# Squares of x summed on TensorE, decay and beta columns as one stationary tile with two passes, softmax sums spread by transposes

## The chip, the cores and the metric

The kernel runs on one core of one Trainium2 chip. The metric is the device time of one execution in microseconds; the kernel before takes 911.56 us (median of 3 runs, 911.46 to 915.03). The profile is that of one execution, taken by the hardware profiler.

## The reference, cut to what matters

One layer of a diffusion backbone, in f32, for 512 latent tokens and 256 context tokens of width 1024. The parts that the change touches:

```python
def rms_norm(x, g):
    xf = x.astype(jnp.float32)
    return xf * lax.rsqrt(jnp.mean(xf * xf, axis=-1, keepdims=True) + EPS) * g.astype(jnp.float32)
...
    h = rms_norm(x, g_norm1) * (1.0 + sc1) + sh1
    hc = rms_norm(ctx, g_norm1) * (1.0 + csc1) + csh1
    aq, ak, av, dq, dk, dv, dz, da, db, ga, gd = split_cols(h @ w_in)
...
        beta = jax.nn.sigmoid(pb.reshape(pb.shape[0], T, N_DIR, DN_HEADS))
        g = -jnp.exp(a_log) * jax.nn.softplus(pa.reshape(pa.shape[0], T, N_DIR, DN_HEADS) + dt_bias)
...
    p = jax.nn.softmax(jnp.concatenate([s_loc, s_ctx, s_sink], axis=-1).astype(jnp.float32), axis=-1)
```

`da` and `db` (16 columns each of the input projection) give the decay g and the rate beta of the gated DeltaNet branch. Behind these come the DeltaNet scans in both directions, windowed attention, gates, an output projection and an MLP.

## The kernel before, in words

Activations lie transposed: 128 features on the partitions, tokens along the free axis, eight feature tiles `kt`. Products of f32 precision are made of three matmuls in a faster 32-bit format: each weight w and each activation x is split in a high part (a cast on ScalarE) and a low part (the difference, on VectorE), and `mm3` (L288 to L296) adds whi·xhi (L293), whi·xlo (L294) and wlo·xhi (L295) into one PSUM accumulator. Matmuls on plain f32 operands (the sums of squares L332 and L676, the modulation products L228, the broadcasts L634) run as two passes each in the trace.

**The start.** 30 matmuls of `ones` on `ones` (L209) keep TensorE busy while the first loads land. The four pieces of `xT` (128x1024 each, two feature tiles) land one after the other. `norm1` (L315) squares each on ScalarE (L319), adds the four on VectorE (L325), folds 1024 to 512 columns (L329) and sums over the partitions with one matmul with `ones` (L332); logarithm and exponential (both at L164) give 1/rms. `ada(kt)` (L220) makes the modulation columns of one feature tile from two halves of `wada1` (L228); `columns` (L241) evicts them (L244), turns them (L249) and writes `modA` and `modS` (L257, L258). `features(kt)` (L341) calls `modulate` (L298): scale on VectorE (L299), shift and high part on ScalarE (L300), low part on VectorE (L301). The context goes through `norm1` too, with two pieces.

**The early tiles.** While the columns of the eight feature tiles come in, three output tiles of the input projection are accumulated k by k: T_AB (decay and beta: 16 columns of `da`, 16 of zeros, 16 of `db`, and 80 of zeros) and the first two DeltaNet key tiles T_DK and T_DK+1. `load_early` (L282) loads and splits their weights. Per k and tile there are three matmuls of 512 columns and three of 256 (latent and context tokens). Then follow the tiles T_DK+2 and T_DK+3, whose weights are loaded and split by `wload` (L263: cast L271, low part L276), and behind them the `selq` matmuls (L734). The accumulator of T_AB is read from PSUM by L697 (add of the bias `dtb`) and L699 (exponential of beta); a chain of logarithms and exponentials on 16 partitions ends in `gb` (L707), which the `selq` matmuls (L734) read. The key tiles are read by `conv` (L655: ScalarE L658, VectorE L659, L660).

**Attention.** For each of eight (query block, kv head) units, `scores` and `outputs` run. `outputs` transposes the probabilities (L613), splits them, multiplies with the values (L602, L603), and then multiplies the result by the inverse softmax sums: for each of four heads, a matmul (L634) with the sums' column, broadcast to 128 columns, as stationary operand, and the identity gives a 128x128 block with the sums along the free axis; VectorE multiplies (L635).

The order of the instructions on each engine is set when the kernel is built, by a scheduler that goes by data dependences, buffers and its own estimate of times; an engine then works through its list in order. `follow` (L198) adds single orderings by hand.

Of the kernel before, what the change touches and what calls it, by code (L numbers as in the profile page):

```python
# [8 lines left out]
F32 = mybir.dt.float32  # L9
F32R = mybir.dt.float32r  # L10
BF16 = mybir.dt.bfloat16
AF = mybir.ActivationFunctionType
# [24 lines left out]
P = 128  # L37
# [24 lines left out]
UPOS, SPOS = [UORD.index(q) for q in range(4)], [SORD.index(q) for q in range(4)]  # L62


T_AK, T_AV, T_AQ, T_AB = 0, 1, 2, 6
T_DK, T_DV, T_DQ, T_DZ = 7, 11, 15, 19
T_GA, T_GD = 23, 31
N_IN = 39

# [41 lines left out]
def tile_layer(ctx: ExitStack, tc: tile.TileContext, I: dict, out: bass.AP, dbg=None):  # L113
# [42 lines left out]
    def act(out_, in_, func, **kw):  # L156

        sets = TABLES.get(func)
        if sets and actg["set"] not in sets:
            head = A.preload_act_table_set(sets[0])  # L160
            for o in actg["ops"]:
                tc.add_manual_dep(head.ins, o.name, nosync, reason="table sets")
            actg.update(set=sets[0], head=head.ins, ops=[head.ins])
        r = A.activation(out_, in_, func, **kw)  # L164
        if sets:
            tc.add_manual_dep(r.ins, actg["head"].name, nosync, reason="table sets")
            actg["ops"].append(r.ins)
        return r
# [110 lines left out]
    early, EARLY = [], {T_AB: 0, T_DK: 0, T_DK + 1: 0}  # L279
    ebufs = []  # L280

    def load_early():  # L282
        bb = alloc(1024), alloc(1024)
        ebufs.extend(bb)
        early.append((wload(I["win"][list(EARLY)[len(early)]], bufs=bb), bank(2)))


    def mm3(acc, w, xs, start=True, stop=True, ks=None):  # L288
        ks = list(range(len(xs))) if ks is None else ks
        n = len(ks)  # L290
        for i, k in enumerate(ks):
            xhi, xlo = xs[i]
            PE.matmul(acc, w[0][:, k, :], xhi, start=(start and i == 0), stop=False)  # L293
            PE.matmul(acc, w[0][:, k, :], xlo, start=False, stop=False)  # L294
            r = PE.matmul(acc, w[1][:, k, :], xhi, start=False, stop=(stop and i == n - 1))  # L295
        return r  # L296

    def modulate(t, src, r, sc, sh, hi, lo, eng=V):  # L298
# [55 lines left out]
        return mm3(acc[:, :512], w, [hx[k]], start=(k == 0), stop=(k == KT - 1), ks=[k])  # L354


    normed = [norm1(xs_, 4, SEQ, rx)]
    follow(w0, normed[0])
    columns(0, rp0)
    features(0)  # L360
# [228 lines left out]
    def outputs(qb, kv):  # L589

        b0, b1, nb, n = span(qb)
        probs, pks = pkd[qb, kv][:2]
        pv = bank()
        cols = [b0 + b for b in range(nb)] + [4, 5]
        last = None

        def values():
            i0, vs, ph = last
            for x, vo in enumerate(vs):
                i = i0 + x  # L600
                v = r32(VS[:, vo * 256 + kv * P:vo * 256 + (kv + 1) * P])
                PE.matmul(pv.ap, v, r32(ph[0][:, x * 512:x * 512 + 512]), start=(i == 0), stop=False)  # L602
                PE.matmul(pv.ap, v, r32(ph[1][:, x * 512:x * 512 + 512]), start=False, stop=(i == len(cols) - 1))  # L603
            for b in ph:
                b.free()

        for i0 in range(0, len(cols), 2):
            vs = cols[i0:i0 + 2]
            m = len(vs) * 512
            pt = bank(len(vs))  # L610
            for x in range(len(vs)):
                for j in range(4):
                    PE.transpose(pt[:, x * 512 + j * P:x * 512 + (j + 1) * P], probs[j][:, (i0 + x) * P:(i0 + x + 1) * P], ident)  # L613
            ph = alloc(m), alloc(m)
            split(pt.ap, ph[0].ap, ph[1].ap)
            pt.free()
            if last:
                values()
            last = i0, vs, ph
            yield  # L620
        values()
        for p in pks:
            p.free()
        if kv == 0:
            yab[qb] = alloc(512)
        ya, r = yab[qb], own[kv]
        A.activation(ya[r], pv[own[1 - kv]], AF.Copy)
        V.tensor_tensor(ya[r], ya[r], pv[r], op=ALU.add)
        pv.free()

        st = pkd.pop((qb, kv))[2]
        rb = bank()
        for j in range(4):
            PE.matmul(rb[:, j * P:(j + 1) * P], st[:, 2, j:j + 1].broadcast_to([P, P]), ident, start=True, stop=True)  # L634
        V.tensor_tensor(ya[r], ya[r], rb[r], op=ALU.mult)  # L635
        rb.free()
        if kv == 1:
            split(ya.ap, Q[0][:, qb].rearrange("p j t -> p (j t)"), Q[1][:, qb].rearrange("p j t -> p (j t)"))
            ya.free()
        yield  # L640
# [53 lines left out]

    t, t2 = alloc(TOK), alloc(TOK)
    ad, mx, be = t[0:16], t2[0:16], gb[32:48]
    V.tensor_scalar(ad, acc[0:16, :TOK], dtb[0:16], None, op0=ALU.add)  # L697
    V.tensor_scalar(mx, ad, 0.0, None, op0=ALU.max)
    act(be, acc[32:48, :TOK], AF.Exp, scale=-1.0)  # L699
    acc.free()  # L700
    act(be, be, AF.Ln, bias=onec[32:48])
    act(be, be, AF.Exp, scale=-1.0)
    A.activation(ad, ad, AF.Abs)
# [980 lines left out]
def pack(i):  # L1684
# [21 lines left out]
    wbd = i["w_br_dn"][0].reshape(8, HD, D)[heads].reshape(512, D)  # L1706
    aqp = aq.reshape(D, 2, 4, HD).transpose(0, 2, 1, 3).reshape(D, 512)
    z16 = np.zeros((D, 16), np.float32)
    ab = np.concatenate([da, z16, db, z16, np.zeros((D, 64), np.float32)], 1)
    a["win"] = blk(np.concatenate([ak, av, aqp, ab, dk, dv, dq, dz, ga, gd], 1))  # L1710
    wba = i["w_br_attn"][0].reshape(2, 4, HD, D).transpose(1, 0, 2, 3).reshape(512, D)
    a["wbr"] = np.stack([blk(wba), blk(wbd)])
    a["wout"] = blk(i["w_out"][0])
# [10 lines left out]
    prm[:, 67:75] = i["attn_sink"][0][None]  # L1724
    prm[:, 75:111] = i["conv_w"][0].reshape(3, 12, P).transpose(2, 1, 0).reshape(P, 36)
    prm[0:16, 111] = i["a_log"][0].reshape(-1)
    prm[0:16, 112] = i["dt_bias"][0].reshape(-1)

    sel = np.zeros((64, 2, 5, 4, 2), np.float32)
    for n, (kind, places, order) in enumerate(((0, ZP, range(4)), (1, ZP, range(4)), (0, UP, UORD), (1, UP, UORD), (0, (0,) * 4, range(4)))):  # L1730
# [27 lines left out]
```

## Time and profile before

| | |
|---|---|
| median of 3 runs | 911.56 us |
| span of the profiled execution | 909.7 us |
| TensorE, weight loads, VectorE, ScalarE busy | 96%, 79%, 72%, 55% |
| loads | 103.87 MB read, 2.10 MB written, mean 116 GB/s |

The span is from the first to the last instruction of the profiled execution; the profile has no time of its own for that execution beside it, and the median of the timed runs is 1.9 us above the span. A matmul's start is exact, its end is modelled, so TensorE's rate is read from start to start. A row of the timeline gives start, duration, engine, line, operation, output<-inputs, shape, count, and in brackets the idle time before it with what ended it. "L293" is line 293 of the kernel before. A row of the chain of waits gives start, length and what was waited for. A row of the busy time by stretch gives, for each engine, busy time and count, then the granted TensorE clock, the share of the DMA engines, and GB/s.

### The profile page before, as it was taken

What the parts mean: (1) busy time and instruction counts of PE and PEld (TensorE: products, weight loads), DVE (VectorE), ACT (ScalarE), POOL (GpSimd) and SP (SyncE); (2) the same over time, 40 slices, a digit from 0 to 9 for tenths busy, and PEclk for the clock granted to TensorE, in tenths of its full rate; (3) what the DMA queues carried; (4) which work ended last, traced back from release to release, by engine and by line L of the source; (5) the groups of instructions that cost most, each with busy time, mean ns of one, the idle gap of its engine ahead of it and who ended that gap; (6) DMA issues with size and microseconds to landing.
All of it is one profiled execution on the core that took longest, in us unless ns stands there. A gap on an engine that the chain in (4) does not pass through costs nothing.

```text
span 909.7 us, 18033 instructions
## 1 busy us (share of the span) xinstructions
PE 873.9 (96%) x7564; PEld 721.3 (79%) x7564; DVE 652.9 (72%) x1111; ACT 496.9 (55%) x881; POOL 26.0 (3%) x42
## 2 busy tenths in 40 slices
PE   8999999989999998889999999999999999999998
PEld 6688667867777676656677789888898899889986
DVE  5665799876778999566666968896587567837631
ACT  6368764475768795475654434463265246424520
POOL 0000001010000001100000000000000000000000
PEclk9999999999999999999999999999999999999999
DMA  9824455532311136523143645453412332334031
GB/s 355 312 76 117 94 131 107 113 73 47 57 36 35 59 121 235 182 67 99 49 152 107 241 127 186 155 170 115 139 48 93 116 116 70 116 93 139 1 116 46
DMA packets 31985, 107.13 MB, mean 118 GB/s; under 512 B 4000, under 2 KB 4512, under 8 KB 31904
## 3 DMA queue, kind: packets, MB, share of 16 engines
q1 hardware_dynamic: 29600, 97.59, 32.1%
q0 software_dynamic: 2304, 8.39, 5.8%
q8 instruction: 59, 0.97, 0.4%
q14 instruction: 22, 0.18, 0.1%
HBM read 103.87 MB, written 2.10 MB: 116 GB/s over the span
## 4 chain that ended last, share of the span: by engine, by line
PE 60%; DVE 20%; ACT 11%; DMA 6%; issue 3%; SPq 0%; ACTq 0%; DVEq 0%
PE banks L293 12%; PE banks L294 12%; PE banks L295 12%; PE banks L1509 11%; PE banks L1040 5%; DMA m<-in_wada 3%; ACT m L164 2%; DVE m L865 2%; DVE m L864 2%; DVE m L1105 2%; DVE m L204 2%; DMA m<-in_wm 1%; DVE wl L276 1%; ACT m L928 1%; DVE m L875 1%
## 5 line engine op out<-in xcount | busy, mean ns | idle before, releaser
L293 PE MATMUL banks<-m,wh 128*128 128x512 f32 (+1 forms) x568 | 213.2, 376 | 0.5 <-ACT m L203 0.5
L294 PE MATMUL banks<-m,wh 128*128 128x512 f32 (+1 forms) x568 | 210.7, 371 | 0.3 <-DVE m L204 0.2
L295 PE MATMUL banks<-m,wl 128*128 128x512 f32 (+1 forms) x568 | 209.8, 370 | 0.0
L271 ACT ACTIVATE wh<-wr 128x1024 fp32r<-128x1024 f32 (+1 forms) x92 | 90.6, 987 | 130.5 <-PE banks L294 102.5
L1509 PE MATMUL banks<-m,m 128*128 128x256 f32 x1008 | 123.2, 284 | 0.9 <-ACT m L203 0.6
L1509 PEld LDWEIGHTS banks<-m,m 128*128 128x128 f32 x1008 | 121.9, 192 | 2.4 <-ACT m L203 1.2
L203 ACT ACTIVATE m<-m 128x512 fp32r<-128x512 f32 (+2 forms) x118 | 81.9, 719 | 75.0 <-DVE m L1487 12.0
L293 PEld LDWEIGHTS banks<-m,wh 128*128 128x128 f32 x568 | 107.0, 189 | 19.2 <-ACT m L203 1.0
L294 PEld LDWEIGHTS banks<-m,wh 128*128 128x128 f32 x568 | 107.0, 188 | 18.8 <-DVE m L204 1.2
L295 PEld LDWEIGHTS banks<-m,wl 128*128 128x128 f32 x568 | 106.9, 188 | 18.6 <-issue 0.7
L1040 PE MATMUL banks<-m,wh 128*128 128x512 f32 x320 | 108.2, 409 | 3.5 <-ACT m L164 3.5
L204 DVE TENSOR_TENSOR m<-m,m 128x512 fp32r<-128x512 f32 (+2 forms) x118 | 92.3, 804 | 22.3 <-ACT m L203 14.1
L276 DVE TENSOR_TENSOR wl<-wr,wh 128x1024 fp32r<-128x1024 f32 (+1 forms) x76 | 84.2, 1110 | 14.9 <-ACT wh L271 12.6
L1636 DVE SCALAR_TENSOR_TENSOR m<-banks,modT,m 128x512 f32<-128x512 f32 x32 | 24.0, 750 | 68.6 <-PE banks L295 68.4
L1040 PEld LDWEIGHTS banks<-m,wh 128*128 128x128 f32 x320 | 59.6, 190 | 16.5 <-ACT m L164 4.0
L1040 PE MATMUL banks<-m,wl 128*128 128x512 f32 x160 | 65.5, 410 | 0.0
L1105 DVE SCALAR_TENSOR_TENSOR m<-m,m 128x1024 f32<-128x1024 f32 x32 | 38.8, 1220 | 14.3 <-DMA m<-in_wada 14.2
L293 PE MATMUL banks<-m,m 128*128 128x256 f32 (+1 forms) x136 | 44.9, 344 | 1.4 <-ACT m L300 1.2
L294 PE MATMUL banks<-m,m 128*128 128x256 f32 (+1 forms) x136 | 45.1, 340 | 0.9 <-DVE m L301 0.8
L295 PE MATMUL banks<-m,m 128*128 128x256 f32 (+1 forms) x136 | 44.6, 337 | 0.0
L164 ACT ACTIVATE m<-banks,st 128x512 f32<-128x512 f32 (+1 forms) x32 | 23.5, 738 | 24.7 <-DVE st L570 24.4
L1040 PEld LDWEIGHTS banks<-m,wl 128*128 128x128 f32 x160 | 30.5, 190 | 6.5
(258 smaller groups left out, 1339.5 us busy)
## 6 DMA issues: line engine op xcount, KB each, us to landing
m<-in_wada SPq DMA_DIRECT2D x48, 512.0 KB, 5.3
wr<-in_wm SPq DMA_DIRECT2D x40, 512.0 KB, 3.6
wr<-in_win SPq DMA_DIRECT2D x39, 512.0 KB, 3.7
m<-in_wm SPq DMA_DIRECT2D x24, 512.0 KB, 3.9
wl<-in_win POOLq DMA_DIRECT2D x16, 512.0 KB, 5.6
m<-in_xT SPq DMA_DIRECT2D x8, 512.0 KB, 5.6
wr<-in_wbr SPq DMA_DIRECT2D x16, 256.0 KB, 2.6
wr<-in_wout SPq DMA_DIRECT2D x8, 512.0 KB, 3.8
```

Of the source, the lines that this page charges most:

```text
L164: r = A.activation(out_, in_, func, **kw)
L203: A.activation(r32(hi), src, AF.Copy)
L204: (eng or V).tensor_tensor(r32(lo), src, hi, op=ALU.subtract)
L271: upper[0] = A.activation(r32(hi), raw, AF.Copy)
L276: V.tensor_tensor(r32(lo), raw, hi, op=ALU.subtract)
L293: PE.matmul(acc, w[0][:, k, :], xhi, start=(start and i == 0), stop=False)
L294: PE.matmul(acc, w[0][:, k, :], xlo, start=False, stop=False)
L295: r = PE.matmul(acc, w[1][:, k, :], xhi, start=False, stop=(stop and i == n - 1))
L1040: PE.matmul(acc.ap, w[x][:, k, :], hx[k][y], start=(k == p == 0), stop=(k == KT - 1 and p == 2))
L1105: V.scalar_tensor_tensor(wa.ap, wa.ap, 0.5, scr.ap, op0=ALU.mult, op1=ALU.mult, accum_out=modT[:, grp, j:j + 1])
L1509: PE.matmul(dst, r32(self.w[w][i][:, k * P:(k + 1) * P]), xs7[x][k][j], start=(n == 0), stop=(n == 11))
L1636: V.scalar_tensor_tensor(xn_[ct], accs[ct].ap, modT[:, 3, ct:ct + 1], xn_[ct], op0=ALU.mult, op1=ALU.add)
```

## The change

- `norm_x` takes the place of `norm1` for x: each of the four pieces is squared, its two halves of 512 columns are added on VectorE, and a matmul with `ones` adds it into one PSUM bank. Of the last piece VectorE squares one half and ScalarE the other.
- The 64 columns of decay and beta are loaded alone (`wab`, 256 KB). High part and low part lie side by side in one stationary tile of 128 columns, so that two matmuls (with xhi and with xlo) make all products; rows 0 to 63 of the accumulator hold the high part's, rows 64 to 127 the low part's. ScalarE copies the upper rows to SBUF, VectorE adds the two, and the chain to `gb` reads the sum. One buffer of 1024 columns fewer is taken for it. The term wlo·xlo, which `mm3` leaves out, is now included.
- In `outputs` the four matmuls with the identity become transposes of the broadcast columns.

In the built order the change also moves: `norm_x`'s first three matmuls stand right behind the 30 `ones` matmuls, ahead of `ada(0)`; on SP, the load of `tri` stands ahead of the weight loads of T_DK+2 and T_DK+3 instead of behind them; on ScalarE, the casts of these two weight tiles stand behind the copy of the upper rows. There are 16 matmuls fewer in the early tiles and 3 more for the squares. Some matmuls of attention and some VectorE instructions up to the DeltaNet scans change places. From there on the order is the same.

```diff
-T_AK, T_AV, T_AQ, T_AB = 0, 1, 2, 6
+T_AB, T_AK, T_AV, T_AQ = -1, 0, 1, 2
...
+    def wload_ab():
+
+        raw = wp.tile([P, KT, P], F32, tag="wr", bufs=NWR, name=nm("wr"))[:, :4].rearrange("p k (h c) -> p (k h) c", h=2)
+        nc.sync.dma_start(out=raw, in_=I["wab"])
+        b = alloc(1024)
+        ebufs.append(b)
+        w = b.ap.rearrange("p (k c) -> p k c", k=KT)
+        upper[0] = A.activation(r32(w[:, :, :CH]), raw, AF.Copy)
+        V.tensor_tensor(r32(w[:, :, CH:]), raw, w[:, :, :CH], op=ALU.subtract)
+        return r32(w), None
+
     def load_early():
+        if not early:
+            early.append((wload_ab(), bank(2)))
+            return
...
-            PE.matmul(acc, w[0][:, k, :], xlo, start=False, stop=False)
-            r = PE.matmul(acc, w[1][:, k, :], xhi, start=False, stop=(stop and i == n - 1))
+            end = stop and i == n - 1
+            r = PE.matmul(acc, w[0][:, k, :], xlo, start=False, stop=(end and w[1] is None))
+            if w[1] is not None:
+                r = PE.matmul(acc, w[1][:, k, :], xhi, start=False, stop=end)
...
-    normed = [norm1(xs_, 4, SEQ, rx)]
+    def norm_x():
+        ss = bank()
+        for i in range(4):
+            b = alloc(1024)
+            src = xs_[:, i * 1024:(i + 1) * 1024]
+            n = 512 if i == 3 else 1024
+            A.activation(b[:, :n], src[:, :n], AF.Square)
+            if i == 3:
+                V.tensor_tensor(b[:, n:], src[:, n:], src[:, n:], op=ALU.mult)
+            V.tensor_tensor(b[:, :512], b[:, :512], b[:, 512:], op=ALU.add)
+            PE.matmul(ss.ap, ones, b[:, :512], start=(i == 0), stop=(i == 3))
+            b.free()
+        act(rx, ss.ap, AF.Ln, bias=epsc, scale=1.0 / D)
+        ss.free()
+        return act(rx, rx, AF.Exp, scale=-0.5)
+
+    normed = [norm_x()]
...
-            PE.matmul(rb[:, j * P:(j + 1) * P], st[:, 2, j:j + 1].broadcast_to([P, P]), ident, start=True, stop=True)
+            PE.transpose(rb[:, j * P:(j + 1) * P], st[:, 2, j:j + 1].broadcast_to([P, P]), ident)
...
-    V.tensor_scalar(ad, acc[0:16, :TOK], dtb[0:16], None, op0=ALU.add)
+    ab = t2[64:128]
+    A.activation(t2[0:64], acc[64:128, :TOK], AF.Copy)
+    V.tensor_tensor(ab, t2[0:64], acc[0:64, :TOK], op=ALU.add)
+    acc.free()
+    V.tensor_scalar(ad, ab[0:16], dtb[64:80], None, op0=ALU.add)
...
-    act(be, acc[32:48, :TOK], AF.Exp, scale=-1.0)
-    acc.free()
+    act(be, ab[32:48], AF.Exp, scale=-1.0)
```

More of the change, by code (lines that the diff above doesn't have):

```diff
@@ L62 @@
 UPOS, SPOS = [UORD.index(q) for q in range(4)], [SORD.index(q) for q in range(4)]
-T_AK, T_AV, T_AQ, T_AB = 0, 1, 2, 6
-T_DK, T_DV, T_DQ, T_DZ = 7, 11, 15, 19
-T_GA, T_GD = 23, 31
-N_IN = 39
+T_AB, T_AK, T_AV, T_AQ = -1, 0, 1, 2
+T_DK, T_DV, T_DQ, T_DZ = 6, 10, 14, 18
+T_GA, T_GD = 22, 30
 class Buf:
@@ L1708, in pack @@
     z16 = np.zeros((D, 16), np.float32)
-    ab = np.concatenate([da, z16, db, z16, np.zeros((D, 64), np.float32)], 1)
-    a["win"] = blk(np.concatenate([ak, av, aqp, ab, dk, dv, dq, dz, ga, gd], 1))
+    ab = np.concatenate([da, z16, db, z16], 1)
+    a["wab"] = np.ascontiguousarray(ab.reshape(KT, P, 64).transpose(1, 0, 2))
+    a["win"] = blk(np.concatenate([ak, av, aqp, dk, dv, dq, dz, ga, gd], 1))
     wba = i["w_br_attn"][0].reshape(2, 4, HD, D).transpose(1, 0, 2, 3).reshape(512, D)
@@ L1726, in pack @@
     prm[0:16, 111] = i["a_log"][0].reshape(-1)
-    prm[0:16, 112] = i["dt_bias"][0].reshape(-1)
+    prm[64:80, 112] = i["dt_bias"][0].reshape(-1)
     sel = np.zeros((64, 2, 5, 4, 2), np.float32)
```

## The prediction

> **What bounds the kernel now.** I read the page first (span, the chain that ended last), then the busy time by stretch, then the timelines of the three stretches that the change touches.
>
> ```profile
> span 909.7 us, 18033 instructions
> PE 60%; DVE 20%; ACT 11%; DMA 6%; issue 3%; SPq 0%; ACTq 0%; DVEq 0%
> ```
>
> ```profile
> core 0: us, PE busy (x) PEld busy (x) DVE busy (x) ACT busy (x) POOL busy (x), PEclk, DMA share, GB/s
> 24.00:58.00 34.00, 34.00 (x250) 25.40 (x250) 22.95 (x48) 13.93 (x26) 1.47 (x2) 1.00 0.63 229
> 58.00:75.00 17.00, 17.00 (x97) 14.52 (x96) 9.24 (x16) 16.77 (x24) 1.00 (x1) 1.00 0.27 92
> 103.00:177.00 74.00, 69.57 (x589) 55.21 (x589) 71.91 (x143) 41.19 (x62) 6.90 (x8) 1.00 0.53 118
> 203.00:270.00 67.00, 64.62 (x381) 51.18 (x380) 47.35 (x86) 44.77 (x83) 2.60 (x4) 1.00 0.26 51
> 270.00:290.00 20.00, 19.35 (x101) 15.24 (x100) 15.89 (x27) 15.90 (x27) 0.00 (x0) 1.00 0.12 30
> ```
>
> TensorE carries 60% of the chain, but not evenly. From 24 to 75 us it never rests; in 58 to 75 ScalarE (16.77 of 17.00) is as full. From 103 to 177 VectorE is the bound (71.91 of 74.00): TensorE time saved there is worth nothing, but a whole stage that starts earlier or later moves VectorE's start with it. In the attention stretch (203 to 270) TensorE leads again, and 270 to 290 is shared. The change touches four places: the start, the early tiles up to 58 us, the hand-over to the next weights behind them, and attention.
>
> **1. The start: squares summed by TensorE.**
>
> ```profile
> 1.07 9.69 PE L209 MATMUL banks<-ones 128*128 128x128 f32 x60 [1.07 <-DVE ones L174]
> 9.44 1.06 ACT L319 ACTIVATE m<-m 128x1024 f32<-128x1024 f32 x1 [0.16 <-DMA m<-in_xT]
> 10.79 0.64 PE L228 MATMUL banks<-m,m 128*32 128x256 f32 x8
> 11.99 0.64 PE L228 MATMUL banks<-m,m 128*32 128x256 f32 x8 [0.56 <-DMA m<-in_wada]
> 12.70 0.38 ACT L244 ACTIVATE m<-banks 128x256 f32<-128x256 f32 x1 [2.21 <-PE banks L228]
> 12.83 1.10 PE L332 MATMUL banks<-m,ones 128*128 128x512 f32 x2 [0.20 <-DVE m L329]
> 13.96 0.69 ACT L164 ACTIVATE m<-banks,epsc 128x512 f32<-128x512 f32 x1 [0.88 <-PE banks L332]
> 15.35 0.75 DVE L299 SCALAR_TENSOR_TENSOR m<-m,modA,m 128x512 f32<-128x512 f32 x1 [0.56 <-ACT m L164]
> 16.78 1.99 ACT L319 ACTIVATE m<-m 128x1024 f32<-128x1024 f32 x2
> 18.80 1.22 DVE L325 TENSOR_TENSOR m<-m,m 128x1024 f32<-128x1024 f32 x1 [0.62 <-ACT m L319]
> 19.98 0.38 ACT L244 ACTIVATE m<-banks 128x256 f32<-128x256 f32 x1 [1.21 <-PE banks L228]
> 21.13 0.28 DVE L257 TENSOR_SCALAR modA<-banks,bada,c_prm 128x2 f32<-128x2 f32 x1
> 23.14 0.50 PE L293 MATMUL banks<-m,m 128*128 128x512 f32 x1
> ```
>
> ```profile
> 81.75 1.29 PE banks L676 x4
> ```
>
> Now one f32 matmul (L332, two passes) sums the squares after three VectorE adds of 1024 columns and one of 512. The change adds 512 columns to 512 per piece and gives each of four pieces its own f32 matmul; the last square is cut in half between ScalarE and VectorE. VectorE's side gets faster: the last sum is ready about 11.3 us (square ended 10.50; half a square, a multiply and an add of 0.7 us each after the landing at 9.4) in place of 12.83. TensorE's side does not. In the built order of the changed program, the first three sums stand behind the 60 warm-up passes, which end at about 10.7, and ahead of the first half of L228; the fourth stands between its halves. By the L676 row, four passes (one matmul of 512 and one of 256 columns) take 1.29 us, so 0.86 a sum. So: 10.7 + 3 x 0.86 = 13.3; half of L228 0.5, 13.8; the fourth sum issues until 14.7; the logarithm starts 1.13 after the sum's start (12.83 to 13.96), at 15.0; L299 could follow 1.39 later (13.96 to 15.35), at 16.4. The second half of L228 ends at about 15.4, not 12.63, its eviction L244 starts at 15.5, and the columns' L257 follows an eviction by 1.15 (19.98 to 21.13), at 16.7; L299 needs them too and starts at about 17.0. Against 15.35 that is 1.6 us late. The slip passes on: ScalarE squares the context after L300 (16.78), VectorE adds them (18.80) ahead of the second L257 (21.13) in its own queue, and from there L299 and L300 lead to 23.14, from where TensorE is dense. Bounds: +0.8, the logarithm's delay alone (15.0 against 13.96 less what the shorter halves give), to +2.1, with the first columns' 1.68 from L244 to L257 in place of 1.15. I take **+1.6**. The early weight tile's DMA is halved (256 KB less); I cost this at nothing, because after the slip weights land before their turn. The shorter cast and subtract of that tile lie beside it.
>
> **2. One pass less for decay and beta.**
>
> ```profile
> 50.60 0.40 PE L293 MATMUL banks<-m,m 128*128 128x512 f32 x1
> 50.83 0.40 PE L294 MATMUL banks<-m,m 128*128 128x512 f32 x1
> 51.07 0.39 PE L295 MATMUL banks<-m,m 128*128 128x512 f32 x1
> 51.30 0.28 PE L293 MATMUL banks<-m,m 128*128 128x256 f32 x1
> 51.41 0.28 PE L294 MATMUL banks<-m,m 128*128 128x256 f32 x1
> 51.53 0.28 PE L295 MATMUL banks<-m,m 128*128 128x256 f32 x1
> 51.65 0.40 PE L293 MATMUL banks<-m,m 128*128 128x512 f32 x1
> ```
>
> A k-step of a tile with three passes takes 1.05 us (50.60 to 51.65), start to start 0.23 for 512 columns and 0.12 for 256. The third pass goes in eight steps: 8 x (0.23 + 0.12) = 2.8. The first 512 of them ran before 23.14, where TensorE waited anyway, and a few lie where it still waits for features; the rest is on the path. Between 1.9 and 2.8; I take **-2.4**.
>
> **3. The next tiles' weights behind the new fold.**
>
> ```profile
> 51.49 1.99 ACT L271 ACTIVATE wh<-wr 128x1024 fp32r<-128x1024 f32 x2
> 56.98 1.63 ACT L658 ACTIVATE m<-banks,c_prm 128x512 f32<-128x512 f32 x3 [3.49 <-PE banks L294]
> 59.25 0.80 ACT L164 ACTIVATE m<-banks 16x768 f32<-16x768 f32 x1
> 74.77 1.05 ACT L658 ACTIVATE m<-banks,c_prm 128x512 f32<-128x512 f32 x2
> ```
>
> ```profile
> 52.57 2.36 DVE L276 TENSOR_TENSOR wl<-wr,wh 128x1024 fp32r<-128x1024 f32 x2
> 56.05 1.00 DVE L697 TENSOR_SCALAR m<-banks,c_prm 16x768 f32<-16x768 f32 x1 [1.12 <-PE banks L295]
> ```
>
> Now ScalarE casts both next weight tiles (T_DK+2, T_DK+3) at 51.49 while it has nothing else; they are ready before TensorE wants them at 57.95. In the changed order the two casts stand behind the new copy of 64x768 from the decay tile, which waits for that tile's last matmul: first the copy, then the convolution's L658, then the first cast, then an exponential, then the second cast. On SP the load of `tri` now goes ahead of these two weight loads; they are issued while TensorE is still in the early tiles, so I cost that at nothing. With a the moment when the decay accumulator is ready: copy 0.8 (by L164 of 16x768, 0.80), L658 0.6, cast 1.0: first weights at a+2.6. TensorE has two more tiles' last steps, 2.1 us, so it stands idle from about a+1.9 to a+2.6: 0.7. It then runs four matmuls (0.7 us), and the fifth needs the second cast: a+2.6 plus exponential 0.9 plus cast 1.0 is a+4.5, against a+3.4: 1.1 more. The low parts (VectorE's add of 64x768 from PSUM, by L697 1.0, a convolution part, then 1.2 for L276) are ready at about a+4.2, just inside. Sum **+1.8**. Bounds: +0.9 (the copy as short as half L164) to +2.8 (every step late by a semaphore's latency, low parts last). ScalarE gains 0.8 us of copy in a full stretch, but TensorE's own stall leaves it room before 74.77, where it now starts L658 as the tile ends; it has about 0.8 us to spare by the same adding. The chain from decay to `gb` is some twelve steps of at most 1 us on ScalarE and VectorE, and TensorE asks for its end only after 16 more k-steps of 1.05 us and the stalls, at about a+20: nothing.
>
> Parts 1 to 3 give +1.0 at 75 us; VectorE's stretch from 103 starts so much later.
>
> **4. Broadcasts by transposes.**
>
> ```profile
> L634 PE MATMUL banks<-c_ident,st 128*128 128x128 f32 x64 | 8.8, 278 | 0.0
> ```
>
> ```profile
> 211.03 0.98 PE banks L634 x8
> 259.95 0.89 PE banks L634 x8
> 266.61 0.87 PE banks L613 x8
> ```
>
> L634 is 32 f32 matmuls in 64 passes, eight passes (about 0.9 us) a block. A transpose is one pass: L613's eight take 0.87, 0.109 each. So a block falls from 8 passes to 4, 0.44 less, 3.5 in all for eight blocks. Half the blocks lie on the chain (211.03 the first, 259.95 the last of four); the rest lie beside ScalarE and VectorE. Bounds 0 and -3.5; I take **-1.8**. The scheduler also reorders some matmuls between 236 and 290 and some VectorE work up to 360 us; same work, counted 0 with 2 us either way.
>
> [...]
>
> **Sum.** +1.6 - 2.4 + 1.8 - 1.8 = -0.8: span 908.9. The median is 911.56, 1.9 above the profiled span, and I keep that: **910.8 us**.
>
> **Rivals.**
> - *The savings count whole.* All eight blocks are on the path (-3.5), the third pass gives -2.8, the start slips only 0.8 and the casts cost 0.9: -4.6, 907.0; with the reordering's 2 us, 905. For it: TensorE leads the chain. Against: the orders of parts 1 and 3 are fixed in the built program. Chance 0.19.
> - *The queue behind the copy decides, slower.* ScalarE's order makes the next tiles wait at 55 us: price +2.8, start +2.1, third pass -1.9, blocks 0, because the 270 to 290 stretch and ScalarE's exponentials set attention's pace: +3.0, 914.6. It decides from the point where TensorE's stall at the first use of the second weights exceeds the 2.4 saved. Chance 0.16, a quarter of it beyond 916.
> - *Clock.* The clock was halved once, where TensorE had thinned out:
>
> ```profile
> 330.00:350.00 20.00, 18.32 (x165) 14.26 (x164) 19.78 (x34) 15.56 (x35) 2.07 (x4) 0.91 0.42 134
> ```
>
> 0.09 of 20 us is 3.6 us at half clock, at most 1.8 us of work. If transposes do not hold the clock up, attention could see two such dips: -0.8 + 3.6 = +2.8, 914.4. Against: 203 to 270, which holds L613's transposes, shows 1.00. Chance 0.04. [...]
> - *The third pass stays or matmuls are not removed*: the built order has the 16 fewer; chance 0.01, 913.
>
> **Range and chances.** Forecast 0.60, 908 to 913.5 by itself. The range takes in most of both rivals: **905.5 to 914.5**. About 0.5% (4.6 us) is what a measurement of this kernel tells from no change: faster than 907.0 0.18, slower than 916.1 0.06, between 0.76.
>
> **What would show it.** Start: a logarithm at about 15.0 (13.96 now) and a first dense matmul at about 24.7. Early tiles: decay ready about 1 us earlier than 56.05. Hand-over: two gaps on TensorE, about 0.7 and 1.1, at 56 to 60 us, ended by ScalarE's casts; without them I am wrong by 1.8. `selq` matmuls at about 76, not 75.0. Attention: blocks of four at 0.44. Wrong if the warm-up passes end earlier, if features limit TensorE after 24 us, or if the reordering in 236 to 290 moves by more than 2 us.

## The result and the profile after

The changed kernel takes **915.95 us** (median of 4 runs, 915.83 to 917.38); the kernel before took 911.51 us beside it (median of 4). The ratio is 1.0054, with a 95% interval of 1.0033 to 1.0076. In a second series (e13 below) it was 917.21 against 912.92 us, ratio 1.0059 (1.0035 to 1.0083). I had forecast 910.8 us, so 4.4 us of loss stand where 0.8 us of gain was expected.

The page of the changed kernel, its span and the shares of the chain that ended last:

```profile
span 914.3 us, 17946 instructions
...
PE 62%; DVE 19%; ACT 11%; DMA 4%; issue 3%; ACTq 0%; DVEq 0%; SPq 0%
```

TensorE's share rose by 2 points though it has fewer matmuls. The busy time by stretch, the same stretches as before (columns as there):

```profile
core 0: us, PE busy (x) PEld busy (x) DVE busy (x) ACT busy (x) POOL busy (x), PEclk, DMA share, GB/s
24.00:58.00 34.00, 34.00 (x244) 23.71 (x244) 21.52 (x47) 14.04 (x28) 1.47 (x2) 0.97 0.55 203
58.00:75.00 17.00, 15.34 (x87) 13.08 (x86) 12.55 (x20) 16.82 (x22) 1.01 (x1) 1.00 0.37 121
103.00:177.00 74.00, 69.64 (x587) 55.16 (x586) 71.23 (x143) 43.29 (x67) 6.37 (x8) 1.00 0.51 116
203.00:270.00 67.00, 62.04 (x357) 48.87 (x356) 46.70 (x85) 44.30 (x82) 3.40 (x4) 0.97 0.22 48
270.00:290.00 20.00, 19.38 (x100) 14.94 (x98) 14.85 (x21) 16.74 (x30) 0.06 (x1) 1.00 0.22 41
330.00:350.00 20.00, 17.99 (x195) 13.90 (x194) 19.20 (x37) 16.68 (x36) 2.07 (x4) 0.93 0.45 145
```

Two things are new. From 58 to 75 us TensorE rests for 1.66 us (17.00 less 15.34), where it never did before. And the granted clock, 1.00 in the first five stretches before, is 0.97 in two of them.

To see where the time went, I compare the start of the same instruction in both traces at three places. Timelines of before, then of the changed kernel (start, duration, engine, line):

```profile
75.01 1.19 PE L734 MATMUL banks<-c_selq,m 64*64 64x40 f32 x34
337.87 0.11 DVE L870 MEMSET m<- 128x64 f32 x1
429.96 0.16 DVE L1565 TENSOR_TENSOR sh<-modT 128x4 f32<-128x4 f32 x1
```

```profile
77.21 1.01 PE L768 MATMUL banks<-c_selq,m 64*64 64x40 f32 x28
340.86 0.11 DVE L904 MEMSET m<- 128x64 f32 x1
435.30 0.16 DVE L1599 TENSOR_TENSOR sh<-modT 128x4 f32<-128x4 f32 x1
```

So the changed kernel is 2.2 us late when the early tiles are done (forecast +1.0), 3.0 late at 338 us, behind attention (forecast -0.8), and 5.3 late at 430 us, in a stretch where TensorE works in the same order in both (some instructions of VectorE and ScalarE stand elsewhere, up to about 370 us). At the end it is 4.6 late (914.3 against 909.7).

### The profile page after: what moved, and what is told of

It is laid out like the page before. It is cut to its first block, busy times and chain, and to the rows that moved or that the text cites. A ratio compares the mean times of both kernels' runs of the same rounds, so it can differ in the third digit from the quotient of the medians.

```text
span 914.3 us, 17946 instructions
## 1 busy us (share of the span) xinstructions
PE 875.9 (96%) x7522; PEld 719.3 (79%) x7522; DVE 652.1 (71%) x1113; ACT 496.5 (54%) x882; POOL 26.0 (3%) x42
## 4 chain that ended last, share of the span: by engine, by line
PE 62%; DVE 19%; ACT 11%; DMA 4%; issue 3%; ACTq 0%; DVEq 0%; SPq 0%
PE banks L306 11%; PE banks L308 11%; PE banks L310 11%; PE banks L1543 10%; PE banks L1074 8%; ACT m L163 2%; DMA m<-in_wm 2%; DVE m L203 2%; DVE m L899 2%; DVE m L898 2%; DVE wl L275 2%; ACT wh L270 1%; DMA m<-in_wada 1%; ACT m L202 1%; PE banks L644 1%
## 5 line engine op out<-in xcount | busy, mean ns | idle before, releaser
L1074 PE MATMUL banks<-m,wh 128*128 128x512 f32 x320 | 110.6, 416 | 5.5 <-ACT m L163 2.9
L203 DVE TENSOR_TENSOR m<-m,m 128x512 fp32r<-128x512 f32 (+2 forms) x118 | 92.4, 806 | 22.0 <-ACT m L202 13.9
L306 PE MATMUL banks<-m,m 128*128 128x256 f32 (+1 forms) x136 | 45.4, 350 | 0.6 <-ACT m L315 0.6
L308 PE MATMUL banks<-m,m 128*128 128x256 f32 (+1 forms) x136 | 44.7, 341 | 0.1
L310 PE MATMUL banks<-m,m 128*128 128x512 f32 (+1 forms) x120 | 39.7, 339 | 0.0
L163 ACT ACTIVATE m<-banks,st 128x512 f32<-128x512 f32 (+1 forms) x32 | 23.5, 739 | 22.8 <-DVE st L601 22.7
```

The source lines that it names most:

```text
L203: (eng or V).tensor_tensor(r32(lo), src, hi, op=ALU.subtract)
L308: r = PE.matmul(acc, w[0][:, k, :], xlo, start=False, stop=(end and w[1] is None))
L310: r = PE.matmul(acc, w[1][:, k, :], xhi, start=False, stop=end)
L1074: PE.matmul(acc.ap, w[x][:, k, :], hx[k][y], start=(k == p == 0), stop=(k == KT - 1 and p == 2))
```

## The experiments

All runs in one table: the start of the three instructions above, as a difference to the kernel before, from one trace each; then the difference of the medians and the ratio with its 95% interval. The table shows why one trace is not enough: the traces differ from the medians by up to 5 us (e11's profiled execution took 917.33 us, its median is 912.45).

| run | 75 us | 338 us | 430 us | median | ratio |
|---|---|---|---|---|---|
| changed kernel | +2.20 | +2.99 | +5.34 | +4.4 | 1.0054 (1.0033 to 1.0076) |
| e1 squares alone | +1.67 | +1.55 | +4.05 | +2.0 | 1.0014 (1.0000 to 1.0028) |
| e2 transposes alone | +0.20 | +0.97 | 0.00 | +0.6 | 1.0001 (0.9984 to 1.0017) |
| e3 two-pass tile alone | +0.15 | +0.07 | +1.35 | +2.2 | 1.0020 (1.0005 to 1.0034) |
| e4 changed, without squares | +2.38 | +3.01 | +8.21 | +6.9 | 1.0073 (1.0052 to 1.0093) |
| e5 new attention order alone | +2.80 | +4.01 | +3.23 | +1.4 | 1.0019 (1.0008 to 1.0030) |
| e6 transposes, old order | -0.20 | -1.38 | -1.39 | -0.9 | 0.9985 (0.9973 to 0.9997) |
| e7 changed, old order | +1.82 | +0.63 | +1.05 | +2.9 | 1.0024 (1.0011 to 1.0037) |
| e8 changed, casts first | -0.71 | -1.56 | +0.57 | +2.9 | 1.0036 (1.0019 to 1.0053) |
| e9 changed, length restored | +1.46 | +2.15 | +1.78 | +2.0 | 1.0018 (1.0007 to 1.0029) |
| e10 before, length shifted | +0.05 | -0.06 | +2.30 | +1.7 | 1.0016 (0.9998 to 1.0034) |
| e11 parts mended | 0.00 | -1.25 | +1.93 | 0.0 | 1.0004 (0.9988 to 1.0020) |
| e12 mended, length restored | -1.50 | -2.69 | -1.57 | -2.5 | 0.9976 (0.9958 to 0.9995) |
| e13 changed kernel again | +2.54 | +3.32 | +6.04 | +4.3 | 1.0059 (1.0035 to 1.0083) |
| e14 mended, start filled | -0.22 | -1.48 | -0.30 | -1.8 | 0.9984 (0.9971 to 0.9997) |
| e15 all three mended | -0.72 | -1.96 | -1.01 | -2.5 | 0.9982 (0.9967 to 0.9997) |

**My first theory** was the granted clock: the changed kernel's trace has four windows of 3.41 us more than the trace before in which TensorE's granted clock is 0.5 ("half clock"). Its own start at 22.7, 244.6, 347.0, 370.9 and 398.2 us, 65, 30, 7 and 8 times 3.413 us apart, so I take 3.413 us as the length of the clock's windows; one more begins at 913.6, cut off by the end. The trace before has one from 344.7 us, behind a window with 1.82 us of work, and one from 907.9 that the end cuts off:

```profile
341.32:344.73 3.41, 1.82 (x36) 1.49 (x37) 3.41 (x6) 3.30 (x6) 1.57 (x4) 1.00 0.25 102
344.73:348.14 3.41, 3.41 (x9) 2.64 (x9) 3.41 (x3) 0.40 (x1) 0.50 (x1) 0.50 0.51 159
```

The rivals were the slips and gaps of the prediction, and transposes that don't hold the clock, which no trace showed.

### e1 to e4: the parts alone

e1 is the kernel before with `norm_x` in place of `norm1` for x, e2 with the transposes only, e3 with the two-pass tile only (its load, the two matmuls, the copy and the add); e4 is the changed kernel with `norm1`:

```diff
-    normed = [norm_x()]
+    normed = [norm1(xs_, 4, SEQ, rx)]
```

Expected: e1: 

> The kernel before with norm_x alone. Theory (clock windows): the later context sum leaves TensorE idle between 15 and 23 us, one window of 3.41 us is under half full, and the next runs at half clock; together with the slip this costs 1.8 to 2.5 us at 75 us, and 2 to 3 at the end. Rival 1 (slip only, as in the prediction): +1.6 at 75 us, no half clock before 300 us. Rival 2 (the start is not the cause): within 0.5 of the kernel before at 75 us and at the end.

e2: 

> The kernel before with the transposes alone. Theory (clock windows from a new order): the order in attention changes, TensorE waits over 1 us for VectorE at about 240 us, one window falls under half full and the next runs at half clock; blocks of four take 0.44, and the sum is -0.5 to +1 at 310 us; windows at half clock behind 360 us come or go with the place of the windows, +-2. Rival 1 (the transposes do not hold the clock): half clock behind windows that are over half full but for the transposes, so at 145 to 150 and in 195 to 210 us too, +3 or more. Rival 2 (as in the prediction): -1.8.

e3: 

> The kernel before with the decay and beta tile in two passes alone (order of the start as before). Theory: about -1.3 at 55 us and two gaps ended by ScalarE's casts at 56 to 60 us, so +0.2 to +0.8 at 75 us and +0 to +1 at the end, no new half clock before 300 us. Rival 1 (as in the prediction): -0.6 at 75 us. Rival 2 (this part carries the loss): +2 or more at 75 us.

e4: 

> The changed kernel with the old norm1 for x: transposes and two-pass tile without norm_x. Theory: the parts add up, so at 75 us as in the run of the two-pass tile alone, in attention as with the transposes alone; at the end 0 to +2 against the kernel before. Rival 1 (the start is not the cause): +4.4 as with all three. Rival 2 (as in the prediction, without its +1.6): -2.4.

Measured: e1 is 1.67 late at 75 us with no half clock before 300 us, so my theory fell there, and the prediction's slip of 1.6 stands. In e3 the last matmul of the early tiles starts 1.8 early (55.99 against 57.83), and the casts take it back: +0.15 at 75 us. Its median, +2.2, lies above the 0 to +1 expected, and its trace doesn't show why. e2 is 0.97 late at 338 us instead of early, the theory's upper end; its half clock began at 223.1 us, and none at 145 to 150 or 195 to 210, where transposes that don't hold the clock would have brought it. e4 falls outside everything expected: without a part that costs 1.7 us the kernel is no faster than with it (+6.9 against +4.4; the intervals overlap, so that it is slower isn't shown). At 75 and 338 us it stands as the changed kernel does; it loses another 5.2 us between 338 and 430. The parts don't add up there, so something else is lost that these four runs don't place.

### e5 to e7: the order in attention

The order that the scheduler chose for one kernel is written into another as a chain of orderings on each engine; `PINS` holds the instructions' names in that order:

```diff
         tile_layer(tc, aps, out)
+        by = {i.name: i for i in nc.cur_bb.bb.instructions}
...
+        for pins in PINS:
+            names = [f"I-{n}" for n in pins.split() if f"I-{n}" in by]
+            for a, b in zip(names, names[1:]):
+                tc.add_manual_dep(by[b], a, first, reason="order")
```

e5: 

> The kernel before (sums spread by ordinary matmuls of two passes) with the attention order of the run with the transposes alone written out by hand on all engines. Theory (the new order costs, not the instruction): a wait of over 1 us of TensorE for VectorE at about 240 to 245 us, +1.5 to +3 there, and +0.5 to +2 at 290 us against the kernel before; the end follows. Rival (the order is the same work and costs nothing): within 0.5 of the kernel before at 290 us.

e6: 

> The kernel before with the transposes, and its own attention order written out by hand on all engines. Theory (the new order costs): no wait over 1 us at 240 to 245 us, and -0.5 to -1.8 at 290 us, where the transposes alone in their own order had +0.46. Rival 1 (the saved passes lie beside other work): within 0.3 of the kernel before at 290 us. Rival 2 (transposes do not hold the clock): new windows at half clock between 200 and 290 us, + 1 or more.

e7: 

> The changed kernel with the attention order of the kernel before written out by hand. Theory (the new order costs): at 290 us 0.8 to 2.3 less late than the changed kernel (+2.5 there), and 1 to 2.5 faster at the end at an equal number of windows at half clock. Rival (the order is not the cause): +2.5 at 290 us and +4.4 at the end as before.

Measured between 75 and 338 us: in the old order the transposes gain 1.2 us (e6, -0.20 to -1.38; e7, +1.82 to +0.63); the new order with ordinary matmuls loses 1.2 (e5); the new order with transposes loses 0.8 (e2, and the changed kernel). So in these traces the instruction saves 1.2 and the reordering that it brings costs 1.2 to 2.0. The traces of e2 and of the changed kernel have one window at half clock in this stretch (from 223.1 and from 244.6 us), those of e5, e6 and e7 none; how much of the cost is the clock shows in e8 below. The place is visible. Timelines of the changed kernel, TensorE and then VectorE:

```profile
242.64 0.50 PE L633 MATMUL banks<-m,m 128*128 128x512 f32 x1 [0.47 <-ACT m L202]
244.44 0.67 PE L634 MATMUL banks<-m,m 128*128 128x512 f32 x1 [1.30 <-DVE m L203]
```

```profile
241.78 0.82 DVE L600 TENSOR_REDUCE st<-banks 128x1 f32<-128x640 f32 x1 [0.27 <-PE banks L596]
242.52 0.74 DVE L690 SCALAR_TENSOR_TENSOR m<-banks,c_prm,m 128x511 f32<-128x511 f32 x1
243.18 1.22 DVE L203 TENSOR_TENSOR m<-banks,m 128x1024 fp32r<-128x1024 f32 x1
```

TensorE wants the low part of the transposed probabilities (L203), but VectorE's queue now has a row maximum (L600) and a convolution part (L690) ahead of it. e5 has the same wait of 1.30 us with ordinary matmuls:

```profile
246.08 0.50 PE L668 MATMUL banks<-m,m 128*128 128x512 f32 x1 [1.30 <-DVE m L269]
```

e6 has no such wait and beats the kernel before. e7's trace shows the gain at 338 us, but its median is still +2.9: the profiled execution was the fastest of its twelve (911.62 us), and where the others lose isn't shown.

### e8: the casts ahead of the copy

```diff
-    nc.sync.dma_start(out=tri_.ap, in_=I["tri"])
+    tload = nc.sync.dma_start(out=tri_.ap, in_=I["tri"])
...
+    tc.add_manual_dep(tload.ins, loads[0].ins.name, nosync, reason="order")
...
-    A.activation(t2[0:64], acc[64:128, :TOK], AF.Copy)
+    up = A.activation(t2[0:64], acc[64:128, :TOK], AF.Copy)
+    tc.add_manual_dep(up.ins, upper[0].ins.name, nosync, reason="order")
```

> The changed kernel with the loads of the next two weight tiles ahead of tri's and both their casts ahead of the copy on ScalarE. Theory (as in the prediction, the casts behind the copy cost 1.5): the two gaps of TensorE at 58 to 61 us go, at 75 us +0.5 to +0.9 in place of +2.2, if the start runs at full clock. Rival 1 (the copy then comes late and the chain to gb with it): selq waits, +1.5 to +2.2 at 90 us. Rival 2 (the gaps move to the next weights): no gain at 75 us.

The changed kernel, TensorE's two gaps and ScalarE's queue:

```profile
58.97 0.50 PE L306 MATMUL banks<-m,wh 128*128 128x512 f32 x1 [0.68 <-ACT wh L270]
...
60.92 0.50 PE L306 MATMUL banks<-m,wh 128*128 128x512 f32 x1 [0.98 <-ACT wh L270]
```

```profile
56.24 0.81 ACT L729 ACTIVATE m<-banks 64x768 f32<-64x768 f32 x1 [2.90 <-PE banks L308]
57.29 0.69 ACT L689 ACTIVATE m<-banks,c_prm 128x512 f32<-128x512 f32 x1 [0.23 <-PE banks L310]
57.87 1.05 ACT L270 ACTIVATE wh<-wr 128x1024 fp32r<-128x1024 f32 x1
58.94 0.84 ACT L163 ACTIVATE m<-m 16x768 f32<-16x768 f32 x1
59.81 1.06 ACT L270 ACTIVATE wh<-wr 128x1024 fp32r<-128x1024 f32 x1
```

e8, ScalarE and TensorE at the same place:

```profile
51.93 1.99 ACT L270 ACTIVATE wh<-wr 128x1024 fp32r<-128x1024 f32 x2
...
55.54 0.81 ACT L730 ACTIVATE m<-banks 64x768 f32<-64x768 f32 x1 [1.62 <-PE banks L308]
```

```profile
57.32 0.28 PE L310 MATMUL banks<-m,m 128*128 128x256 f32 x1
57.44 0.40 PE L306 MATMUL banks<-m,wh 128*128 128x512 f32 x1
```

With the casts done at 54 us TensorE goes from the early tiles to the next weights without a gap (57.32 to 57.44). e8 is 0.7 early at 75 us, the changed kernel 2.2 late. Of these 2.9, 0.7 was there at 30 us already (+1.26 against +1.96, by the same comparison of traces), so the casts cost 2.2. That is more than the 1.5 expected, and both rivals fall. But only 1.5 us of it arrive in the median, and the intervals of the two overlap; in e8's trace 2.1 us are lost between 338 and 430.

e8's trace shows one thing more. It has the changed kernel's attention order and the same two waits of TensorE, but the clock's windows lie otherwise: the waits fall into two of them, 2.80 and 2.11 us busy, and the clock stays at 1.00.

```profile
239.74 0.50 PE L634 MATMUL banks<-m,m 128*128 128x512 f32 x1 [0.47 <-ACT m L202]
241.54 0.49 PE L635 MATMUL banks<-m,m 128*128 128x512 f32 x1 [1.30 <-DVE m L203]
```

```profile
236.66:240.07 3.41, 2.80 (x18) 1.84 (x16) 2.53 (x7) 3.38 (x7) 0.00 (x0) 1.00 0.00 0
240.07:243.48 3.41, 2.11 (x15) 1.68 (x14) 2.14 (x4) 2.80 (x5) 0.86 (x1) 1.00 0.25 77
243.48:246.90 3.42, 3.42 (x21) 2.85 (x19) 2.62 (x4) 2.17 (x4) 0.00 (x0) 1.00 0.96 153
```

e8 is 2.91 us ahead of the changed kernel at 75 us, 2.90 at the end of the second wait (241.54 against 244.44) and 4.55 at 338 us. The 1.65 in between come behind the second wait, where the changed kernel has its window at half clock (244.6 to 248.0). So without that window the transposes in the new order still gain 0.85 us (-0.71 to -1.56), 0.3 less than in the old order; with one window in this stretch they lose 0.6 to 0.8 (the changed kernel, e2, e4, e9, e13). Most of what the new order costs the changed kernel is the window that its waits bring.

### e9 and e10: the length of TensorE's instruction stream

At 350 to 380 us TensorE stands still several times with nothing that released it ("issue"). TensorE's timelines, before and then the changed kernel:

```profile
358.43 0.21 PE L895 MATMUL banks<-m,m 32*32 32x32 f32 x1 [1.22 <-issue]
...
370.10 0.18 PE L896 MATMUL banks<-m,m 32*32 32x32 f32 x1 [2.02 <-issue]
```

```profile
360.28 0.18 PE L930 MATMUL banks<-m,m 32*32 32x32 f32 x1 [0.93 <-issue]
...
369.93 0.39 PE L1074 MATMUL banks<-m,wh 128*128 128x512 f32 x1 [2.62 <-issue]
...
375.68 0.21 PE L930 MATMUL banks<-m,m 32*32 32x32 f32 x1 [0.70 <-issue]
```

I counted TensorE's records (matmuls, weight loads, and its few semaphore waits and drains) ahead of each: 6082 and 6593 before, 5825, 6337 and 6594 in the changed kernel. All are 193 or 194 above a multiple of 256, and so are all such stalls of over 0.4 us in all of the traces. The page lists a DMA queue for code:

```profile
q8 instruction: 59, 0.97, 0.4%
```

59 packets of 16 KB, and for each of them the changed kernel has 256 such records (15,104 in all), the kernel before 257 (15,189); in each of the two traces, the stalled matmuls start 1.3 to 1.6 us after such a packet has ended. So the new theory: TensorE's code comes in blocks of 256 instructions, and where transfers are dense (from 353 to 377 us the DMA engines are 0.73 busy before, 0.81 in the changed kernel) and matmuls short (0.2 us) the next block isn't there yet. That it is the dense transfers that hold it up is my guess; no run varies them. The change has 85 instructions fewer on TensorE (15,104 in place of 15,189), so the boundaries fall elsewhere in the program. The stalls in the two timelines above come to 3.2 and 4.3 us.

The test changes nothing but the length: some of the 30 `ones` matmuls of the start become small ones, 25 in e9 (changed kernel, length as before) and 47 in e10 (kernel before, boundaries as in the changed kernel).

```diff
-NONES, NWAIT = 30, 8
+NONES, NWAIT, NTINY = 26, 8, 25
...
+    for n in range(NTINY):
+        q = slice(32 * (n % 4), 32 * (n % 4) + 32)
+        PE.matmul(wb_[q, :32], ones[q, :32], ones[q, :32], start=True, stop=True)
```

e9: 

> The changed kernel with 4 of the 30 ones matmuls at the start replaced by 25 small ones of 32x32, so that TensorE's instruction stream has the length that it has before the change, with the same order of work. Theory (code blocks): the stalls without a releaser at 356 to 377 us stand at every 256th instruction of TensorE; with the length restored they come back to the places of the kernel before, 3.2 us in all in place of 4.25, and the median falls by 1 to 2 us. Rival (the stalls belong to the work or to its DMAs): same stalls at the same lines as in the changed kernel, time within 0.5.

e10: 

> The kernel before with 4 of the 30 ones matmuls replaced by 47 small ones of 32x32, so that its instruction stream stands against blocks of 256 as that of the changed kernel does. Theory (code blocks): the stalls at 356 to 377 us move to the places that they have in the changed kernel, the one ahead of the matmuls of 512 columns takes 2.5 to 3.2 us, 4 to 6 us in all, and the median rises by 0.5 to 2 us. Rival: within 0.5 of the kernel before.

TensorE in e9, then in e10:

```profile
361.58 0.18 PE L932 MATMUL banks<-m,m 32*32 32x32 f32 x1 [2.34 <-issue]
```

```profile
358.01 0.21 PE L899 MATMUL banks<-m,m 32*32 32x32 f32 x1 [1.59 <-issue]
...
367.39 0.50 PE L1043 MATMUL banks<-m,wh 128*128 128x512 f32 x1 [2.51 <-issue]
```

With the length restored, the stall ahead of the matmul of 512 columns (2.62) is gone and one of 2.34 is left in that stretch; between 338 and 430 us the kernel gains 0.4 where the changed one lost 2.35, and the loss in the median is +2.0 in place of +4.4. With the length shifted, the kernel before gets that stall (2.51) at the corresponding line, loses 2.4 between 338 and 430 us, and 1.7 in the median, with an interval that just reaches 1. The loss moves with the length in both directions, and not with the order on VectorE: e9 keeps the changed kernel's order and e10 the old one. Two limits: 0.7 us of e9's lead over the changed kernel stand at 75 us already (+1.46 against +2.20), which code blocks at 350 us can't have made; and the stalls in e9 add up to less than I expected (2.3, not 3.2), so a block's end at the old place doesn't stall each time.

### e11 and e12: parts mended

e8's casts, e6's order, the old `norm1`; e12 also with the length restored (28 small matmuls).

e11: 

> Two-pass tile with both casts ahead of the copy, and transposes in the old attention order, old norm1 for x. Theory (the parts add up as in the runs alone): -2 at 75 us and -3.2 at 290 us against the kernel before; at the end -3 to 0, as code blocks and windows at half clock behind 340 us take some of it back. Rival (what is gained ahead of 340 us is lost there, since transfers set the pace): -3 at 290 us and within 0.7 at the end.

e12: 

> As the run with the parts mended, with TensorE's instruction stream brought to the length of the kernel before by small matmuls in the start. Theory (code blocks): stalls at 356 to 377 us at the places of the kernel before, and 0.5 to 2 us faster than the run without it; -2 to -4 against the kernel before. Rival (transfers set the pace): no difference between the two.

e11 has the median of the kernel before; e12, the same work in the same order with 4 of the 30 `ones` matmuls replaced by 28 small ones, is 2.5 us faster than before (909.98 us), an interval wholly below 1; that speaks against the rival "transfers set the pace", though the two intervals overlap a little. Not all of it is code blocks: the traces are 1.5 us apart at 75 us already, where e11 is at 0.00 and not at the -2 expected. Same order, but e11 has two windows at half clock in a row (6.83 us from 20.0) and e12 one (3.41 us from 22.0).

### e13 to e15: the clock, filling, and the sum

e14 adds five `ones` matmuls in TensorE's wait at 20 us, with 23 small ones in the start in place of 28; e15 is e12's mending with `norm_x`.

```diff
     last[0] = low0
...
+    for _ in range(5):
+        last[0] = PE.matmul(wb_[:, :P], ones, ones, start=True, stop=True)
...
```

e13: 

> The changed kernel itself, unchanged, for more executions and a second trace with the windows of the clock elsewhere. Theory (windows of 3.41 us that are under about 0.54 full bring half clock, and their place against the kernel differs by execution): the trace has half clock behind each window that is under 0.54 full, and behind no other, at other places than before if the windows stand elsewhere; median 914.5 to 916.5, so that 3 of the 4.4 us stay with twelve executions. Rival (the clock dips belong to the kernel's own places): half clock at 22.7, 244.6, 347, 371 and 398 us again.

e14: 

> As the run with the parts mended and the length restored, but five of the small matmuls' worth of instructions moved: five ones matmuls of 128 columns (1.1 us) stand in TensorE's wait for the context's sums at about 20 us. Theory (half full windows bring half clock, and the removed third pass left this one empty): no half clock at 20 to 26 us, 0.4 to 0.7 less late at 30 us than the run without them (+0.47 there), and 0.3 to 0.8 faster at the end. Rival (the filling delays the work behind it as much as it gains): no difference.

e15: 

> All three parts, each mended: norm_x, two-pass tile with both casts ahead of the copy, transposes in the old attention order, length of TensorE's instruction stream restored. Theory (the parts add up): the run with the parts mended and the length restored plus norm_x, which cost 1.67 at 75 us and 0.7 at the end alone: 910.5 to 912. Rival (norm_x is free when the rest is mended): 910 as without it.

e13: half clock began at 23.5, 245.4, 347.8 and 371.6 us, where the first trace had 22.7, 244.6, 347.0, 370.9 and 398.2. The grid of windows stood 0.7 later, and the same thin places of the program were hit, but for the last: the window from 395.5 us was 0.49 full, under the 0.54 that I had named, and brought none. (0.54 is an estimate: it lies between a window 0.53 full in the trace before, 1.82 of 3.41, which half clock followed, and one 0.56 full in the changed kernel's, 1.90 of 3.41, which it didn't.) So both halves of my sentence were wrong as alternatives: the windows move and the places stay. The loss stayed (+4.3), at 917.21 us, above the 914.5 to 916.5 expected. e14: no half clock at 20 to 26 us, as expected, but two windows of it from 13.2 us, behind the thinned `ones`, and the kernel came out of the start 1.3 us later than e12. Its median is 911.12 against 909.98: a gain isn't shown. e15: 910.44 us; `norm_x` costs 0.8 at 75 us (-0.72 against -1.50) and nothing that the median tells from e12, as the rival said.

## Why the prediction was wrong

**The failed steps** are two. One is the sentence "The scheduler also reorders some matmuls between 236 and 290 ...; same work, counted 0 with 2 us either way": in the traces it cost 1.2 to 2.0 us, all on the bad side; in the changed kernel about 0.3 of that is the new waits and 1.65 the window at half clock that follows them (e8). The other was no sentence at all: the sum ended at 290 us, as if an equal order of TensorE behind it meant equal time. Between 338 and 430 us the changed kernel lost 2.35 us more. With the length of TensorE's stream restored that loss is gone (e9, 0.4 gained there), and with the length shifted the kernel before has it (e10, 2.4 lost), so I put it down to the ends of code blocks that fell elsewhere. The stalls themselves are only 1.0 us longer in sum (4.25 against 3.24); the traces of the changed kernel and of e10 also have two windows at half clock there (370.9 and 398.2; 368.3 and 395.6) that the trace before doesn't have.

Point by point:

- *Start, +1.6*: right; 1.67 alone (e1). The steps were off against each other: the logarithm started at 14.46, not 15.0, and L299's counterpart at 16.58, not 17.0.

```profile
14.46 0.69 ACT L163 ACTIVATE m<-banks,epsc 128x512 f32<-128x512 f32 x1 [4.30 <-PE banks L382]
...
16.58 0.75 DVE L314 SCALAR_TENSOR_TENSOR m<-m,modA,m 128x512 f32<-128x512 f32 x1
```

- *Third pass, -2.4*: -2.0 (e8, +1.26 at 30 us, by the same comparison, to -0.71 at 75).
- *Casts behind the copy, +1.8*: right in mechanism and place, two gaps of 0.68 and 0.98 (forecast 0.7 and 1.1); 2.2 in all (e8), 2.0 in e3.
- *Transposes, -1.8*: -1.2 in the old order (e6, e7); four took 0.48 (213.13 to 213.61), where eight passes took 0.98 before: half, as the sum had it (0.44).

```profile
213.13 0.64 PE L665 MATMUL banks<-c_ident,st 128*128 128x128 f32 x4
213.61 0.38 PE L644 MATMUL banks<-c_ident,m 128*128 128x128 f32 x2
```

- *Sum of the trace*: 1.7 - 2.0 + 2.2 = 1.9 at 75 us; 0.3 more, which I put down to the half clock at 22.7 us without a run for it, gives 2.2; attention +0.8 (transposes -1.2, new order +2.0); 338 to 430 us +2.35; behind that -0.7; together 4.6.
- *The rival "clock"* (0.04) had the effect and the wrong cause. I cut all 17 traces into the clock's own windows of 3.413 us and took TensorE's modelled busy share in each. Of 31 windows at full clock that were under 0.49 full, 29 were followed by one at half clock; of 32 between 0.49 and 0.56, 16; of over 4300 above, 2. Transposes count as busy in this: 32 windows were over 0.56 full with transposes and under 0.49 without, and none brought half clock. Three pairs from the changed kernel, the window and the one behind it:

```profile
19.28:22.70 3.42, 1.53 (x14) 0.86 (x7) 2.62 (x6) 1.92 (x3) 0.00 (x0) 1.00 1.02 412
22.70:26.11 3.41, 3.41 (x14) 1.69 (x14) 3.32 (x6) 1.69 (x4) 0.00 (x0) 0.51 1.03 422
241.18:244.59 3.41, 1.64 (x10) 1.09 (x11) 3.11 (x6) 3.38 (x4) 0.00 (x0) 1.00 0.00 0
244.59:248.00 3.41, 3.41 (x14) 2.82 (x14) 0.53 (x2) 1.74 (x4) 0.86 (x1) 0.50 0.58 124
193.39:196.80 3.41, 1.90 (x12) 1.45 (x11) 2.81 (x6) 3.12 (x8) 1.15 (x3) 1.00 0.00 0
196.80:200.22 3.42, 3.42 (x141) 2.51 (x139) 1.86 (x4) 3.31 (x7) 0.00 (x0) 1.00 0.02 5
```

1.53 and 1.64 us of work in a window bring 0.51 and 0.50 in the next; 1.90 us do not, and of these only 1.27 are not transposes. That transposes do not hold the clock up, the condition of the rival with 0.04, does not agree with these windows. What thinned the windows were waits: the context's sums in the start, VectorE's queue in attention, the code blocks at 367 us.

How much of the 4.4 us is the clock can be bounded only. A least-squares fit over all 292 executions, one constant per kernel, gives 0.64 us (0.57 to 0.71) of time for each us of lost clock (span times one less the mean granted clock). The changed kernel lost 9.0 us (11 executions), the kernel before 4.9 (119): 2.6 us go with the clock. They are not beside the waits above but partly the same loss, since a wait empties the window that the half clock follows. By itself one window cost 1.65 us in attention (the changed kernel against e8), nearly the 1.7 us of clock that it takes (half of 3.41). Two in a row cost 2.8 in the start: e5 has the start of the kernel before, half clock lasted 6.83 us from 19.9, and it was 2.8 late at 75 us, where e2 and e6, with the same start at full clock, and e10, with small matmuls in it, were between -0.2 and +0.2.

- *Range*: 905.5 to 914.5 held e12 and not the change. I had counted a slower rival at the hand-over (914.6) at 0.16, but gave the order and everything behind 290 us no price of their own. Open is why e4 loses more behind 338 us than the changed kernel; its stalls there add up to 5.9 us (1.87, 3.16 and 0.83) by the same boundaries, and half clock lasts 6.83 us from 374.1, but its length wasn't varied. Open too is e1, which keeps the old order and loses 2.5 us between 338 and 430 with stalls of 2.75, less than the 3.24 of the kernel before: code blocks don't explain all that is lost there.

## What to carry to other kernels

When an edit changes an instruction that a scheduler costs, treat the new order as a change of its own and price it: in the changed kernel's traces it cost more than the edit saved (2.0 against 1.2 us), and writing out the old order gave the saving back (e6, e7). Before judging an edit of a few us in a long kernel, look at whether stalls without a releaser stand at one place modulo 256 instructions, as they did here (193 or 194), and restore the length as a control. And where the granted clock falls behind TensorE's waits, read them twice, once for the wait and once for the window behind it: here 1.77 us of waits at 241 to 244 us, then a window at 0.50 that cost 1.65.

## What the runs showed of the hardware that was not expected

- Stalls at every 256th of TensorE's records: where they came, 0.5 to 4.4 us each at 354 to 377 us (e11's longest was 4.37), with the DMA engines 0.73 (before) to 0.84 (e9) busy from 353 to 377; e9 had one of 1.05 us at 203.6 us too.
- The clock's windows stood elsewhere in each of the 17 traces (between 0.2 and 3.4 us against the span's start, modulo 3.413), and the same two waits were followed by half clock or not as they fell: in the changed kernel into one window, 1.64 of 3.41 us busy, and the next ran at 0.50; in e8 into two, 2.80 and 2.11 busy, and the clock stayed at 1.00. The kernel before ran from 909.57 to 916.05 us; by the fit, part of that spread goes with the clock.
- Waits in two pieces were enough: behind 1.30 and 0.47 us at 241 to 244 us, together 1.77 of a window of 3.41, the next was granted 0.50 (the changed kernel).
